# A batched matmul whose last store moves behind its critical sections, and whose second load of b moves to ScalarE's queue

## The chip, the cores and the metric

One core of a Trainium2 chip. The metric is the device time of one execution in microseconds (us); "ratio" is the mean time of one kernel's fast runs over the mean of the other kernel's fast runs of the same rounds, so it is not quite the ratio of the medians that are quoted. In the experiments the ratios come out when each kernel's first run, the profiled one, is left out; the medians and differences have it in, so the two can differ by some 0.1 us.

## The reference

```python
batch, m, k, n = 16, 512, 512, 512        # a: (batch, m, k), b: (batch, n, k), float32
np.matmul(a, b.transpose(0, 2, 1)).astype(np.float32)
```

Sixteen products of 512 x 512 matrices. 33.5 MB are read and 16.8 MB written.

## The kernel before

The batches are taken in pairs. A load brings two batches of a or of b (2 MB); loads 0, 2, 4, ... are of a and 1, 3, 5, ... of b. VectorE casts to bf16, TensorE transposes and multiplies, ScalarE evicts the products to `ob`, and stores of 1 MB carry them out. The streams of all engines stand in one large critical section, in which the framework inserts no waits and the kernel counts semaphores itself. A second small section at the end waits for the last store. These are the parts that matter here:

```python
    NL = 7                                 # slots for loads
    NO = 7                                 # slots for outputs
    STORES = "SSSSOSOSOSSOOOOOO"           # GpSimd: S stores, O hands a free output slot to ScalarE
    SW = 5
    LATE = {11: (8, 9), 13: (10, 11), 15: (12, 13)}
    # ... (cut)
    with tc.tile_critical(no_gpsimd_drain=True):
        # ... (cut: buffers, semaphores, load(), landed())
        def store(n):
            engine = nc.gpsimd if n < STORES.count("S") else nc.sync
            engine.wait_ge(s_out, n + 1)
            engine.dma_start(
                out[n].rearrange("(p j) n -> p j n", j=J), ob[:, n % NO]
            ).then_inc(landed(n)[0], 16)

        load(0)
        load(1, nc.scalar)
        for n in range(2, NL):
            load(n)
        for n in range(2 * pairs):
            nc.sync.wait_ge(s_ld[n % NL], 16 * (n // NL + 1)).then_inc(s_go, 1)
            if n > 0 and n + NL - 1 < 2 * pairs:
                load(n + NL - 1)           # waits until VectorE has cast what was in the slot
            for m in LATE.get(n, ()):
                store(m)
        store(batch - 2)
        store(batch - 1)
        for n in range(batch - NO, batch - 1):
            nc.sync.wait_ge(*landed(n))
        # ... (cut: GpSimd's, VectorE's, ScalarE's and TensorE's streams)

    with tc.tile_critical(no_gpsimd_drain=True):
        nc.sync.wait_ge(*landed(batch - 1))
```

Of the kernel before, what the change touches and what calls it, by code (L numbers as in the profile page):

```python
# [10 lines left out]
def kernel(  # L11
# [6 lines left out]
    nc = tc.nc  # L18
    P = 128
    batch, M, K = a.shape  # L20
    _, N, _ = b.shape
    J = M // P
# [6 lines left out]
    NL = 7  # L29
    NO = 7  # L30
# [7 lines left out]
    def sbuf(name, shape, dtype):  # L38
        return ctx.enter_context(nc.sbuf_tensor(name, shape, dtype))
# [4 lines left out]
    with tc.tile_critical(no_gpsimd_drain=True):  # L44
# [8 lines left out]
        ob = sbuf("ob", [P, NO, J, N], f32)  # L53
# [27 lines left out]
            out=ident[:], in_=ident[:], compare_op=mybir.AluOpType.not_equal, fill=1.0,  # L81
# [6 lines left out]
        def load(n, engine=nc.sync):  # L88
            u, slot = n // 2, n % NL
            src = (a if n % 2 == 0 else b)[2 * u:2 * u + 2].rearrange(  # L90
                "e (p j) k -> (e p) j k", j=2 * J
            )
            if n >= NL:

                nc.sync.wait_ge(s_cd, n - NL + 2)
            engine.dma_start(ld[:, slot], src).then_inc(s_ld[slot], 16)

        def landed(n):

            if n < STORES.count("S"):  # L100
                return s_st[n % SW], 16 * (n // SW + 1)

            slot = (n - STORES.count("S") + 2) % NL
            return s_ld[slot], 16 * (len(range(slot, 2 * pairs, NL)) + 1 + (n - STORES.count("S") >= NL))
# [7 lines that stand above are left out]

        load(0)
        load(1, nc.scalar)
        for n in range(2, NL):
            load(n)
        for n in range(2 * pairs):
            nc.sync.wait_ge(s_ld[n % NL], 16 * (n // NL + 1)).then_inc(s_go, 1)
# [3 lines left out]
            for m in LATE.get(n, ()):  # L122
                store(m)
        store(batch - 2)
        store(batch - 1)
        for n in range(batch - NO, batch - 1):
            nc.sync.wait_ge(*landed(n))


        n_st = n_of = 0  # L130
# [20 lines left out]
        with nc.Fori(0, pairs, engines=[dve]) as u:  # L151
            for x, (h, w, s_c, s_w) in enumerate(
# [4 lines left out]
                if x == 0:  # L157
# [3 lines left out]
                    out=h[:, :J, :], in_=src[:, :J, :HK]  # L161
                ).then_inc(s_cd, 1)
                nc.vector.tensor_copy(  # L163
                    out=h[:, J:, :], in_=src[:, J:, :HK]
                ).then_inc(s_c, 1)
                nc.vector.tensor_copy(out=w[:], in_=src[:, :, HK:]).then_inc(s_w, 1)  # L166
            for ko in range(KO):
# [5 lines left out]
                if ko == 1:  # L173
# [3 lines left out]
                    out=tb[:, ko, :],  # L177
# [4 lines left out]
        act = nc.scalar.engine  # L182
# [4 lines left out]
        with nc.Fori(0, pairs, engines=[act]) as u:  # L187
            for ko in range(KO):
# [5 lines left out]
                for e in range(2):  # L194
                    c = nc.scalar.copy(  # L195
                        out=ta[:, ko, e * J * P:(e + 1) * J * P].rearrange(
                            "k (j p h) -> k j p h", j=J, h=2
                        ),
# [5 lines left out]
            for e in range(2):  # L204
                take(s_of, 1)
                dst = ob[:, bass.ds((u * 2 + e) % NO, 1)].rearrange("m o j n -> m (o j) n")
                for j in range(J):
                    if j < J - 1:
                        nc.scalar.wait_ge(s_mm, j + 1)
                    else:  # L210
# [3 lines left out]
                        out=dst[:, j, :].rearrange("m (p j) -> m p j", j=2 * J),  # L214
# [50 lines left out]
                                t.then_inc(s_mm, 1)  # L265


    with tc.tile_critical(no_gpsimd_drain=True):
        nc.sync.wait_ge(*landed(batch - 1))


# [28 lines left out]
```

## Time and profile before

| | us |
|---|---|
| median of 6 runs | 125.48 (125.31 to 125.68) |
| span of the profiled run | 123.55 |
| first packet of data | 1.94 |
| last semaphore of the last store | 122.22 |
| from there to the end of the span | 1.33 |

The prediction below shows the slices, the stretches and the waits on which the reading rests. In the rows of slices each digit is the busy share, in tenths, of one of 40 equal slices of the span. "DMA share" is the mean busy share of the 16 DMA engines. A transfer has landed when the last increment of its semaphore has come; most transfers here get 16, one from each DMA engine. The exit of the second section shows as records of SyncE's sequencer at the line that opens it, L268. The view of that line has: line, engine (a "q" marks the sequencer), operation, count, shortest/median/longest in ns, first and last start in us.

```profile
L268 SPq NOP  x2: 13/13/13, 120.3 to 122.6; - x2
L268 SPq EVENT_SEMAPHORE  x1: 17/17/17, 122.4 to 122.4; - x1
L268 SPq DRAIN  x1: 7/7/7, 122.5 to 122.5; - x1
```

The first NOP, at 120.3 us, is the entry. Signal, drain and second NOP, at 122.4, 122.5 and 122.6 us, are the exit. They last 7 to 17 ns each, but they come one after the other behind the landing at 122.22 us, the signal 0.15 us after the branch before it, the others at distances of some 0.08 us. What they cost is the distance.

### The profile page before, as it was taken

How to read it: one execution, taken by the hardware profiler on the slowest of the kernel's cores; microseconds unless marked ns; L12 is line 12 of the kernel's file. 1: busy time of each engine (PE TensorE's matmuls, PEld its weight loads, DVE VectorE, ACT ScalarE, POOL GpSimd, SP SyncE). 2: the span in 40 equal slices, each digit the busy share in tenths (PEclk: the TensorE clock that was granted, in tenths of full speed). 3: DMA queues.
4: the chain of work that ended last, by engine and by line, in shares of the span. 5: the costliest groups of instructions: out<-in, count | busy, mean ns of one | idle time of the engine just before them, and what ended most of it. 6: DMA issues, size and time to landing. Idle time of an engine off the chain costs nothing. (4 is left out here: it accounts for less than half of the span.)

```text
span 123.5 us, 2364 instructions
## 1 busy us (share of the span) xinstructions
PE 90.7 (73%) x768; PEld 55.8 (45%) x768; DVE 67.9 (55%) x96; ACT 68.1 (55%) x130; POOL 5.9 (5%) x14
## 2 busy tenths in 40 slices
PE   0000089999899999989998999899999946994000
PEld 0000079546734774476467447644764535441000
DVE  0000597891898389568928991894787078400000
ACT  4000063458946885595769558937876069555000
POOL 2000000000000160001010230000000000000000
PEclk9999999999999999999999999999999999999955
DMA  4999999999999999999999999999999999999990
GB/s 127 419 446 435 424 424 430 424 424 424 430 430 435 424 403 385 461 390 427 454 400 454 424 414 454 411 432 446 416 438 419 416 427 422 430 424 427 430 385 11
DMA packets 4608, 50.33 MB, mean 407 GB/s; under 512 B 512, under 2 KB 512, under 8 KB 512
## 3 DMA queue, kind: packets, MB, share of 16 engines
q1 hardware_dynamic: 3312, 39.85, 76.2%
q0 software_dynamic: 1152, 8.39, 16.1%
q10 hardware_dynamic: 144, 2.10, 4.3%
HBM read 33.55 MB, written 16.78 MB: 407 GB/s over the span
## 5 line engine op out<-in xcount | busy, mean ns | idle before, releaser
L255 PE MATMUL ps<-tb,ta 128*128 128x512 bf16 x256 | 57.8, 379 | 0.5
L213 ACT COPY ob<-ps 128x512 f32 x64 | 34.5, 588 | 28.5 <-PE ps L255 24.6
L195 ACT COPY ta<-tp 128x512 bf16<-128x512 bf16 x64 | 32.8, 610 | 15.4 <-PE tp L236 15.4
L255 PEld LDWEIGHTS ps<-tb,ta 128*128 128x128 bf16 x256 | 24.1, 97 | 30.7 <-issue 4.0
L236 PE MATMUL tp<-ident,ha 128*128 128x128 bf16 x256 | 19.6, 230 | 19.3 <-PEq L141 19.3
L236 PEld LDWEIGHTS tp<-ident,ha 128*128 128x128 bf16 x256 | 16.6, 103 | 23.1 <-issue 21.3
L176 DVE COPY tb<-tp 128x1024 bf16<-128x1024 bf16 x32 | 21.2, 684 | 4.8 <-DVEq L141 4.8
L236 PE MATMUL tp<-ident,hb 128*128 128x128 bf16 x256 | 18.1, 227 | 2.2 <-PEq L141 2.2
L236 PEld LDWEIGHTS tp<-ident,hb 128*128 128x128 bf16 x256 | 16.1, 102 | 2.6 <-issue 2.6
L160 DVE CAST ha<-ld 128x1024 bf16 x8 | 5.5, 686 | 13.7 <-DVEq L141 13.7
L171 DVE COPY ha<-wa 128x2048 bf16<-128x2048 bf16 x8 | 5.5, 692 | 13.6 <-DVEq L141 13.6
L166 DVE CAST wa<-ld 128x2048 bf16 x8 | 9.8, 1227 | 0.0
L166 DVE CAST wb<-ld 128x2048 bf16 x8 | 9.7, 1218 | 0.0
L160 DVE CAST hb<-ld 128x1024 bf16 x8 | 5.5, 688 | 6.4 <-DVEq L141 6.4
L109 POOL DMA_DIRECT2D out_dram<-ob x8 | 5.2, 655 | 65.2 <-DMA ld<-in_b_dram 41.1
L175 DVE COPY hb<-wb 128x2048 bf16<-128x2048 bf16 x8 | 5.5, 684 | 0.1
L163 DVE CAST ha<-ld 128x1024 bf16 x8 | 5.5, 686 | 0.0
L163 DVE CAST hb<-ld 128x1024 bf16 x8 | 5.5, 683 | 0.0
L186 ACT ACT_TABLE_LOAD x1 | 1.3, 1283 | 1.5 <-SPq L44 1.5
L80 POOL TENSOR_SCALAR_AFFINE_SELECT ident<-ident 128x128 bf16<-128x128 bf16 x1 | 0.3, 282 | 0.2 <-POOL ident L78 0.2
L78 POOL MEMSET ident<- 128x128 bf16 x1 | 0.2, 204 | 0.5 <-SPq L44 0.5
L186 ACT COPY one<-const-float32-1.0 128x1 f32<-128x1 f32 x1 | 0.2, 191 | 0.0
(4 smaller groups left out, 0.4 us busy)
## 6 DMA issues: line engine op xcount, KB each, us to landing
ld<-in_a_dram SPq DMA_DIRECT2D x8, 2048.0 KB, 26.3
ld<-in_b_dram SPq DMA_DIRECT2D x7, 2048.0 KB, 29.8
out_dram<-ob POOLq DMA_DIRECT2D x8, 1024.0 KB, 29.0
out_dram<-ob SPq DMA_DIRECT2D x8, 1024.0 KB, 19.6
ld<-in_b_dram ACTq DMA_DIRECT2D x1, 2048.0 KB, 12.2
```

What stands on the lines that cost most here:

```text
L109: engine.dma_start(out[n].rearrange("(p j) n -> p j n", j=J), ob[:, n % NO]).then_inc(landed(n)[0], 16)
L160: nc.vector.tensor_copy(out=h[:, :J, :], in_=src[:, :J, :HK]).then_inc(s_cd, 1)
L163: nc.vector.tensor_copy(out=h[:, J:, :], in_=src[:, J:, :HK]).then_inc(s_c, 1)
L166: nc.vector.tensor_copy(out=w[:], in_=src[:, :, HK:]).then_inc(s_w, 1)
L171: nc.vector.tensor_copy(out=ha[:], in_=wa[:]).then_inc(s_ca, 1)
L175: nc.vector.tensor_copy(out=hb[:], in_=wb[:]).then_inc(s_cb, 1)
L176: nc.vector.tensor_copy(out=tb[:, ko, :], in_=tp[:, 2 + ko % 2].rearrange("k j p -> k (j p)"),).then_inc(s_eb, 1)
L186: nc.scalar.copy(out=one[:], in_=nc.const_aps.tensor(1.0, (P, 1), f32))
L195: c = nc.scalar.copy(out=ta[:, ko, e * J * P:(e + 1) * J * P].rearrange("k (j p h) -> k j p h", j=J, h=2), in_=tp[:, ko % 2, :, e * HP:(e ...
L213: c = nc.scalar.copy(out=dst[:, j, :].rearrange("m (p j) -> m p j", j=2 * J), in_=ps[:, j, :].rearrange("m (j p) -> m p j", j=2 * J),)
L236: t = nc.tensor.transpose(tp[:, 2 * x + g, j, :], h[:, j, g * P:(g + 1) * P], ident[:])
L255: t = nc.tensor.matmul(ps[:, j, :], ta[:, ko, (e * J + j) * P:(e * J + j + 1) * P], tb[:, ko, :].rearrange("k (j p) -> k j p", j=2 * J)[:, ...
```

## The change

The intent is a shorter end: the last store becomes a plain transfer of the framework after both sections, so that the framework's closing wait stands for it and no section has to be left afterwards. ScalarE, idle by then, takes the waits for the stores before it. Besides this the second load of b (load 3) goes to ScalarE's queue, as the first one does already.

```diff
         load(0)
         load(1, nc.scalar)
-        for n in range(2, NL):
+        load(2)
+        load(3, nc.scalar)
+        for n in range(4, NL):
             load(n)
 ...
         store(batch - 2)
-        store(batch - 1)
-        for n in range(batch - NO, batch - 1):
-            nc.sync.wait_ge(*landed(n))
 ...
-    with tc.tile_critical(no_gpsimd_drain=True):
-        nc.sync.wait_ge(*landed(batch - 1))
+    with tc.tile_critical(sync_engine=act, no_gpsimd_drain=True):
+        for n in range(batch - NO, batch - 1):
+            nc.scalar.wait_ge(*landed(n))
+    waits = nc.cur_bb.bb.instructions[-1]
+    last = nc.sync.dma_start(
+        out[batch - 1].rearrange("(p j) n -> p j n", j=J), ob[:, (batch - 1) % NO]
+    )
+    tc.add_manual_dep(
+        last.ins,
+        waits.name,
+        mybir.DependencyInfo(mybir.DependencyClass.NoSync, mybir.DependencyReason.DATA),
+        reason="order of issue",
+    )
```

## The prediction

> **What bounds the kernel now.** I read the page first, then the stretches, the chain, and the waits of SyncE's queue. The page's slices settle the large question: this kernel is bound by its transfers.
>
> ```profile
> PE   0000089999899999989998999899999946994000
> DVE  0000597891898389568928991894787078400000
> DMA  4999999999999999999999999999999999999990
> HBM read 33.55 MB, written 16.78 MB: 407 GB/s over the span
> ```
>
> The 16 DMA engines are busy from the first slice to the last but one, while TensorE and VectorE have holes and end three to six slices early. 50.33 MB are moved. In steady state the bandwidth row stays near 425 GB/s, so the bytes alone are worth 50.33 / 0.425 = 118.4 us of the 123.5 us span. What remains, about 5 us, is the head and the tail. The table by stretches places them (columns: stretch, length, busy time and count of PE, PEld, DVE, ACT, POOL, then clock, DMA share, GB/s):
>
> ```profile
> 0.00:1.90 1.90, 0.00 (x0) 0.00 (x0) 0.00 (x0) 0.42 (x1) 0.69 (x6) 1.00 0.00 0
> 1.90:2.90 1.00, 0.00 (x0) 0.00 (x0) 0.00 (x0) 0.99 (x2) 0.00 (x0) 1.00 1.06 279
> 2.90:13.00 10.10, 0.00 (x0) 0.00 (x0) 0.00 (x0) 0.06 (x1) 0.00 (x0) 1.00 1.02 435
> 13.00:23.00 10.00, 7.22 (x68) 6.52 (x68) 8.06 (x12) 4.11 (x8) 0.00 (x0) 1.00 0.99 423
> ...
> 112.00:120.20 8.20, 0.69 (x4) 0.10 (x1) 0.00 (x0) 1.09 (x2) 0.00 (x0) 0.83 1.00 424
> 120.20:121.80 1.60, 0.00 (x0) 0.00 (x0) 0.00 (x0) 0.00 (x0) 0.00 (x0) 0.50 0.08 31
> 121.80:123.50 1.70, 0.00 (x0) 0.00 (x0) 0.00 (x0) 0.00 (x0) 0.00 (x0) 0.50 0.00 0
> ```
>
> Nothing moves before 1.9 us. From there to 120.2 us the share is 0.99 to 1.06, that is, all engines are always at work. In 120.2 to 121.8 us it is 0.08, a little over one engine in 16: one DMA engine ends about 1.3 us after the other fifteen (in the records of packets its last data ends at 121.75 us, the others' between 120.1 and 120.7). Then 1.7 us in which nothing is moved. These last 3.3 us are the only part of the end that an instruction could shorten.
>
> The chain of work confirms that compute isn't the end. Its last piece in order of time is
>
> ```profile
> 112.89 0.59 ACT ob L213
> ```
>
> so ScalarE's last eviction ends at 113.48 us, ten microseconds before the end. What SyncE's queue waits for afterwards (engine, line, waited for: us in total, times, longest):
>
> ```profile
> SPq L127 <- DMA out_dram<-ob: 5.8, 3, 2.4
> SPq L109 <- ACT ob L213: 1.8, 1, 1.8
> SPq L295 <- DMA out_dram<-ob: 1.7, 1, 1.7
> ```
>
> L127 are the waits for the six stores before the last, inside the first section; L295 is the wait for the last store, in a section of its own. It lasts 1.7 us, so the last store is still under way when SyncE gets there.
>
> The sequencers' records give the end to the hundredth: the last store is issued at 113.50 us; L127 is done at 119.77; the first section is left with a join of all engines (119.81 to 120.36); the wait of L295 runs from 120.54 to 122.24, and the semaphore of the late DMA engine arrives at 122.22. From there: branch 122.28, signal 122.43, drain 122.52, NOP 122.59 (the second section is left), drain 122.63, drain 122.70, and then two barriers of all engines with a clearing of semaphores to 123.55. So 1.3 us follow the landing, and the first 0.4 us of it is the exit from the second section.
>
> **What the Trainium skill says.** "DMA: Bandwidth & Descriptors", section "Issuing engines are not separate DMA queues": DMAs of the scalar, sync and gpsimd engines run on the same 16 DMA engines and interleave; a second issuing engine saves the sequencer's issue time only. The trace agrees: loads 0 and 1, issued on SyncE and ScalarE 0.03 us apart, landed together at 13.29 and 13.12 us, at the same 435 GB/s that one queue alone gets later. The same page, "Queues, rings and completion order": each DMA engine takes turns between its queues packet by packet. This fits too, for two loads of 2 MB in some 10.2 us (2.9 to 13.1) is about twice the 4.89 us between landings of successive loads on one queue. "Perfetto Trace Analysis", section "Per-instruction lifecycle": waiting for a semaphore and its propagation lie outside the profiled window, which is why I read gaps between sequencer records and not their 7 to 33 ns durations.
>
> **The change part by part.**
>
> *Load 3 onto ScalarE's queue.* The number of bytes, of issues and of packets stays. One issue of 0.39 us (ScalarE's own now) moves from SyncE to ScalarE. It delays the table load at 1.48 us by some 0.4 us, but ScalarE's first real work is after 15 us: free. SyncE's loads 4 to 6 are issued 0.4 to 0.5 us earlier, into a queue with over 20 us of work: free. What changes is the order of landing. Now load 2 lands at 18.05 us and load 3 at 22.93. With turns between the two queues, both land near 22.9 to 23.1 us. Does anyone want load 2 earlier? The records of VectorE say no: it works at pair 0 until its loop comes round, and takes the signal for load 2 at 23.05 us, its first cast for pair 1 being at 23.43. So pair 1 starts 0 to 0.2 us later. Load 8, which waits for that cast (issued at 24.14), moves by as much; loads 4 to 7, 8 MB or 19.6 us of work, stand before it. Worth on the end: 0, give or take 0.1 us.
>
> *The waits for stores 9 to 14 move to ScalarE.* ScalarE is done at 113.48 us, so it can sit in them until 119.77 us at no cost; its section's exit, some 0.5 us, ends near 120.3, still 1.9 us before the landing. Off the path.
>
> *The last store behind the sections.* SyncE must first leave the first section. That exit waits for all engines' drains, ScalarE's at 113.48 us being the last, and took 119.96 to 120.36 us on the old trace, 0.4 us. So the store is issued near 113.9 to 114.1 us and not 113.50. This is hidden: the store before it holds the same queue until 118.0 us (landing of its first DMA engines), and from issue to first packet ScalarE's first load took 1.0 us, SyncE's 1.9. Even at 1.9 us it is ready at 116.0, 2 us early. The data still end at 120.2 us, and the late engine at 121.75.
>
> *The end.* Landing at 122.22 as before. The wait belongs to the framework's closing drain, so branch, signal, drain and NOP of the second section are gone from the path: instead of 122.24 to 122.63 to the closing drain, one hop of 0.06 us between adjacent records. Saved: 0.39 - 0.06 = 0.33 us. The two barriers, 0.9 us, stay.
>
> Sum: 0 + 0 + 0 - 0.33 = -0.33 us, so 125.49 - 0.33 = 125.16, and I say 125.15 us.
>
> **The rivals.**
>
> *The last store is held back.* If the framework sets it behind the waits of the second section and not only behind the first, it is issued at 119.8 us or later, when the queue is empty. Then 1.0 us to the first packet, 2.45 us of data (between landings of successive stores: 115.6, 118.0, 120.5) and 0.5 us to the semaphore put the landing at 123.8 to 125, 1.5 to 2.8 us later: 126.6 to 128. For it: the diff needs a dependence by hand to get the order it wants. Against: that dependence is one of order of issue without a semaphore, and the section holds instructions of ScalarE alone. I give this 1 in 20.
>
> *The late DMA engine changes its lag.* It gathers its 1.2 us from slow packets: the first ones (up to 1.45 us for 16 KB against 0.61) and those around 45 us, when GpSimd's stores begin. Two queues in use until 23 us may shift which engine suffers. If all ended together the time would fall by 1.2 us; it can also grow. For it: the time of the very end hangs on that one engine. Against: the three runs of before differ by only 0.2 us, so the lag recurs, and both its sources are untouched. This gives the range its width.
>
> *Compute becomes the bound through the later load 2.* Pair 1 would have to slip by more than the backlog, which is 19.6 us early and 6.7 us (120.2 - 113.5) at the end. A slip of 0.2 us vanishes. I give it nothing.
>
> **Range and chances.** The one certain term is -0.33 us with an error of 0.15; head and middle add perhaps 0.2, the late engine 0.3. Low 124.7, high 125.6. Two per cent would be 2.5 us: a gain of that size is not there, because only 3.3 us after 120.2 are not transfer at full rate, and the closing barriers with the receipt take half; a loss needs the first rival at its worst. Faster 0.01, same 0.97, slower 0.02.
>
> **What would show it.** Right: the slices of DMA as before; loads 2 and 3 landing within 0.5 us of each other near 23 us; VectorE's first cast for pair 1 by 23.7 us; the last store issued before 114.5 us; the landing near 122.2 us, and 0.9 to 1.0 us from there to the end of the span instead of 1.3. Wrong: a gap in the DMA row after 118 us (the store was held), a DMA share in the last stretch very different from 0.08 (the late engine), or as many records as before between the landing and the first closing drain (the framework's own wait costs what the section's exit did).

## The result

The changed kernel took 125.26 us (median of 6 runs, 124.99 to 125.48) against 125.48 us. The ratio is 0.9979 with a 95% interval of 0.9962 to 0.9995, a gain of 0.27 us by the means; in us the interval is a gain of 0.06 to 0.48. The time alone thus tells a gain of 0.33 us from none, but not from one of 0.1; the traces below do. The predicted time was 125.15 us, the range 124.7 to 125.6, the class "within 2%": all hold.

On the page of the changed kernel the large picture is as it was:

```profile
PE   0000079999899999989998999899999929997000
DMA  4999999999999999999999999999999999999990
q1 hardware_dynamic: 3168, 37.75, 72.3%
q10 hardware_dynamic: 288, 4.19, 8.3%
```

The transfers still fill every slice but the ends. The queue of ScalarE (q10) carries 288 packets, two loads, where it carried one (144 packets). The stretches at the end of the changed kernel:

```profile
112.00:120.20 8.20, 1.34 (x7) 0.39 (x4) 0.00 (x0) 1.53 (x3) 0.00 (x0) 0.71 1.01 427
120.20:121.80 1.60, 0.00 (x0) 0.00 (x0) 0.00 (x0) 0.00 (x0) 0.00 (x0) 0.50 0.09 36
121.80:123.40 1.60, 0.00 (x0) 0.00 (x0) 0.00 (x0) 0.00 (x0) 0.00 (x0) 0.50 0.00 0
```

There is no gap before 120.2 us, so the last store was not held back, and the share of 0.09 after it is again mostly one late DMA engine. What SyncE's queue waits for after 112 us, and the exit of the second section, now read:

```profile
SPq L306 <- DMA out_dram<-ob: 7.7, 1, 7.7
SPq L44 <- PEq L44: 0.9, 1, 0.9
SPq L44 <- ACTq L44: 0.7, 1, 0.7
```

```profile
L268 ACTq NOP  x2: 14/14/14, 114.3 to 120.8; - x2
L268 ACTq EVENT_SEMAPHORE  x1: 17/17/17, 120.6 to 120.6; - x1
L268 ACTq DRAIN  x1: 14/14/14, 120.7 to 120.7; - x1
```

SyncE leaves the large section early (two waits of 0.9 and 0.7 us for the drains of TensorE and ScalarE), issues the store at 114.31 us and sits in the framework's closing wait for 7.7 us. The exit of the second section is ScalarE's now and ends at 120.8 us, 1.6 us before the landing at 122.44 us. After the landing come the wait's end at 122.49, two drains at 122.53 and 122.59 us and the two barriers. The end, taken from the records of the two traces ("fifteenth" and "sixteenth" here and in later tables are in the order in which the DMA engines finish, not the engines' numbers):

| | before | changed |
|---|---|---|
| ScalarE's last eviction ends | 113.47 | 114.12 |
| last store issued | 113.50 | 114.31 |
| fifteenth DMA engine done (semaphore) | 121.00 | 121.37 |
| sixteenth DMA engine done (semaphore) | 122.22 | 122.44 |
| from landing to the end of the span | 1.33 | 1.00 |
| span | 123.55 | 123.44 |

The end is 0.33 us shorter. In this pair of profiles the landing is 0.22 us later, which single runs cannot tell from scatter; over the runs of the first series of experiments, the spans of before have a mean of 123.73 us and the changed kernel's are all 123.4.

### The profile page after: what moved, and what is told of

It is laid out like the page before. It is cut to its first block, busy times and chain, and to the rows that moved or that the text cites. A ratio compares the mean times of both kernels' runs of the same rounds, so it can differ in the third digit from the quotient of the medians.

```text
span 123.4 us, 2365 instructions
## 1 busy us (share of the span) xinstructions
PE 91.1 (74%) x768; PEld 56.0 (45%) x768; DVE 68.1 (55%) x96; ACT 68.2 (55%) x130; POOL 5.8 (5%) x14
```

## The experiments

My theory: the whole gain is the exit of a section taken from behind the landing, 0.33 us, and load 3's queue is worth nothing. The rival: the loads on two queues make the gain. A second question is how much room the last store has, since it is now issued later. A third is the DMA engine that ends some 1.1 us after the others, which no part of the change touches but on which the time of the end hangs.

In the tables below "difference" is mean minus mean of the kernel before in the same rounds.

### The two parts alone, and one section more

`after_again` is the changed kernel. `tail_only` takes back the loads:

```diff
-        load(2)
-        load(3, nc.scalar)
-        for n in range(4, NL):
+        for n in range(2, NL):
```

`load_only` is the kernel before with only this part of the change added. `third_section` is the kernel before with its last section written twice:

```diff
     with tc.tile_critical(no_gpsimd_drain=True):
         nc.sync.wait_ge(*landed(batch - 1))
+
+    with tc.tile_critical(no_gpsimd_drain=True):
+        nc.sync.wait_ge(*landed(batch - 1))
```

Expected of `after_again`: 

> The changed kernel once more, on the chip of the next three runs. My theory: 0.2 to 0.4 us below the kernel before (0.9979 before), all of it from the 0.33 us between the landing of the last store and the end of the span. Rival: the gain comes from the loads on two queues, and the end gives nothing.

Expected of `tail_only`: 

> The end of the changed kernel with the loads of the kernel before (only load 1 on ScalarE's queue). My theory: 0.33 us below before, as the whole change or a little better, since the late landing of load 2 is spared; 0.95 to 1.05 us from the landing to the end. Rival (the loads make the gain): same as before, 0.0 us.

Expected of `load_only`: 

> Load 3 on ScalarE's queue, and the end of the kernel before. My theory: within 0.15 us of before, either sign; loads 2 and 3 landing within 0.3 us of each other near 23.4 us. Rival (the loads make the gain): 0.2 to 0.3 us below before.

Expected of `third_section`: 

> The kernel before with one more section at the end that waits again for the last store, which has landed: it pays one more entry and exit. My theory: a section's exit behind the landing costs 0.33 us and its entry 0.2, so 0.4 to 0.6 us above before. Rival (sections cost nothing there): 0.0 us.

| run | median us | ratio to before (95%) | difference | landing to end of span |
|---|---|---|---|---|
| after_again | 125.24 | 0.9980 (0.9967 to 0.9994) | -0.30 | 1.00 |
| tail_only | 125.08 | 0.9962 (0.9949 to 0.9976) | -0.45 | 1.00 |
| load_only | 125.45 | 0.9996 (0.9982 to 1.0010) | -0.08 | 1.33 |
| third_section | 126.36 | 1.0067 (1.0053 to 1.0081) | +0.79 | 1.98 |

The rival falls: with the new end alone the gain is there, with the loads alone it isn't. The last column, from each trace, is 1.00 us wherever the new end is and 1.33 us wherever the old one is. The added section shows the same cost with the sign turned. Its entry and exit come after the landing (122.33 us):

```profile
L271 SPq NOP  x2: 13/13/13, 122.8 to 123.3; - x2
L271 SPq EVENT_SEMAPHORE  x1: 17/17/17, 123.2 to 123.2; - x1
L271 SPq DRAIN  x1: 7/7/7, 123.3 to 123.3; - x1
```

They stretch the end by 0.65 us (1.98 - 1.33), a little more than the 0.6 that I took as the most. The time rose by 0.79 us, outside the 0.4 to 0.6 that I expected. The rest is outside the span: the time less the span is 2.06 us in this kernel's runs (mean of five) and 1.83 us in those of before. What it consists of I can't see.

### How much room the last store has

`hold_14` and `hold_13` are the kernel before with the last store issued only after the landing of an earlier store (number 14 or 13), on purpose:

```diff
-        store(batch - 1)
-        for n in range(batch - NO, batch - 1):
+        for n in range(batch - NO, 15):        # 14 in hold_13
+            nc.sync.wait_ge(*landed(n))
+        store(batch - 1)
+        for n in range(15, batch - 1):         # 14 in hold_13
             nc.sync.wait_ge(*landed(n))
```

Expected of `hold_14`: 

> The kernel before, with the last store issued only after the store before it has landed. It puts my first rival of the prediction to the test, by doing on purpose what I feared the framework would do. I said 1.5 to 2.8 us in the prediction for this case (1.0 us to the first packet, 2.45 us of data, 0.5 us to the semaphore, from 119.8 us on). If the last store has no slack at all, it would be more, some 4 us.

Expected of `hold_13`: 

> The kernel before, with the last store issued one store earlier than in the run with the longer hold: after the landing of the last but two, near 117.4 us instead of 113.5. My theory: the store before it keeps the DMA engines at work to 118.0 us and the late one to 119.2, and the first packet comes 1.0 us after the issue, so at most 0.4 us is lost and, if the late engine decides, nothing: 0.0 to 0.3 us above before. Rival (every us of delay of the last store counts): 3 to 4 us above before.

| run | last store issued | landing | sixteenth after fifteenth | median us | ratio (95%) | difference |
|---|---|---|---|---|---|---|
| before (profile) | 113.50 | 122.22 | 1.21 | | | |
| hold_13 | 117.85 | 122.64 | 0.94 | 125.49 | 0.9992 (0.9973 to 1.0011) | 0.0 |
| hold_14 | 119.98 | 123.82 | 0.03 | 126.97 | 1.0118 (1.0101 to 1.0136) | +1.49 |

Issuing the store 4.4 us later costs nothing that the runs can tell (the interval is -0.34 to +0.14 us). Issuing it 6.5 us later costs 1.5 us. The stretches near the end show why; first `hold_13`, then `hold_14` (the last two columns are DMA share and GB/s):

```profile
118.00:119.00 1.00, 0.00 (x0) 0.00 (x0) 0.00 (x0) 0.00 (x0) 0.00 (x0) 0.50 0.40 164
119.00:120.00 1.00, 0.00 (x0) 0.00 (x0) 0.00 (x0) 0.00 (x0) 0.00 (x0) 0.50 1.10 459
120.00:121.00 1.00, 0.00 (x0) 0.00 (x0) 0.00 (x0) 0.00 (x0) 0.00 (x0) 0.50 1.04 426
121.00:122.00 1.00, 0.00 (x0) 0.00 (x0) 0.00 (x0) 0.00 (x0) 0.00 (x0) 0.50 0.13 49
```

```profile
119.00:120.00 1.00, 0.00 (x0) 0.00 (x0) 0.00 (x0) 0.00 (x0) 0.00 (x0) 0.50 0.02 8
120.00:121.00 1.00, 0.00 (x0) 0.00 (x0) 0.00 (x0) 0.00 (x0) 0.00 (x0) 0.50 0.31 131
121.00:122.00 1.00, 0.00 (x0) 0.00 (x0) 0.00 (x0) 0.00 (x0) 0.00 (x0) 0.50 0.93 393
122.00:123.00 1.00, 0.00 (x0) 0.00 (x0) 0.00 (x0) 0.00 (x0) 0.00 (x0) 0.50 0.97 393
```

In `hold_13` most DMA engines do stand idle between 118 and 119 us (share 0.40), and the time is unchanged all the same: the late engine, done with the store before only at 119.8 us, has no gap, and it alone sets the landing (122.64 us; the fifteenth comes at 121.70). In `hold_14` all are empty, all start the last store together, and the lag is gone with the wait. This is the price of the rival that I gave 1 in 20; the changed kernel's store, 0.8 us later than before, is far inside the room.

### The late DMA engine

`sync_stores` is the changed kernel with GpSimd's eight stores on SyncE's queue:

```diff
-    SW = 5
+    SW = 8
-    LATE = {11: (8, 9), 13: (10, 11), 15: (12, 13)}
+    LATE = {5: (0, 1), 7: (2, 3), 9: (4, 5), 11: (6, 7), 12: (8, 9), 13: (10, 11), 15: (12, 13)}
 ...
-            engine = nc.gpsimd if n < STORES.count("S") else nc.sync
+            engine = nc.sync
 ...
-            if what == "S":
-                store(n_st)
-                n_st += 1
-            else:
+            if what == "O":
```

`last_120` is the changed kernel with its last store cut in two, and `last_skip` is `tail_only` with it cut in four (the dependence by hand moves into the loop; it is cut here):

```diff
-    last = nc.sync.dma_start(
-        out[batch - 1].rearrange("(p j) n -> p j n", j=J), ob[:, (batch - 1) % NO]
-    )
+    for r in (slice(0, 120), slice(120, 128)):   # last_skip: 0:96, 96:117, 117:124, 124:128
+        last = nc.sync.dma_start(
+            out[batch - 1].rearrange("(p j) n -> p j n", j=J)[r], ob[r, (batch - 1) % NO]
+        )
```

Expected of `sync_stores`: 

> The changed kernel with the eight stores that GpSimd issued put on SyncE's queue; GpSimd only waits. It asks whether the DMA engine that ends 1.1 us late in every profile, and the slow packets at 45 to 47 us, come from GpSimd's way of issuing. If so: late engine within 0.5 us of the others, landing near 120.8 us and 1.3 to 1.8 us below before. Rival (an engine is late whoever issues): lag of 1 us as before, and the time of the changed kernel (0.3 us below before), or more if one queue in strict order holds the loads back.

Expected of `last_120`: 

> The changed kernel with the last store cut in two transfers, of 120 and of 8 partitions. By the Trainium skill (DMA: Bandwidth & Descriptors, on how many engines a DMA uses) 120 partitions go to the 15 lowest engines and 8 to the 8 lowest, so the sixteenth engine gets none of the last store. If the late engine is the sixteenth: the last landing 0.8 to 1.1 us earlier, time 1.1 to 1.4 us below before. If it is another: landing 0 to 0.6 us later than in the changed kernel (one packet more on eight engines, 0.31 us, and one issue more).

Expected of `last_skip`: 

> The better end with the loads of before, and the last store cut in four: 96, 21, 7 and 4 partitions. By the Trainium skill's rule for the number of engines, 96 go to all sixteen (6 each), 21 and 7 to the seven lowest (4 more), 4 to the four lowest (1 more). The run with 120 and 8 partitions showed that the late engine is one of the eight lowest; the skill (same page, latency table) says that engines 7 and 15 are usually slower. If the late one is the eighth of them, it has 6 packets instead of 8 (0.61 us less) and the lowest ones up to 11 (0.92 us more): last landing near 121.8 us and not 122.4, lag of the sixteenth under 0.4 us, time 0.3 to 0.5 us below the uncut version. If the late one is among the seven lowest: landing 0.6 to 0.9 us later, near 123.2 us, time 0.6 to 1.0 us above the uncut version.

| run | landing | sixteenth after fifteenth | median us | ratio (95%) | difference |
|---|---|---|---|---|---|
| sync_stores | 126.87 | 0.01 | 129.74 | 1.0348 (1.0308 to 1.0387) | +4.35 |
| last_120 | 123.13 | two transfers, see text | 125.62 | 1.0004 (0.9988 to 1.0020) | +0.14 |
| last_skip | 123.24 | four transfers, see text | 126.12 | 1.0054 (1.0034 to 1.0073) | +0.67 |

`sync_stores` was a miss as a kernel and answers only half of its question. Its page shows a hole near the end that no other kernel has:

```profile
ACT  3000066459567956876069260893409915894630
DMA  4999999999999999999999999999999999993094
```

Early stores stand in one queue behind loads (the first is issued at 37.72 us and lands at 64.88; before, 42.81 and 55.15), outputs' slots come free late, ScalarE and with it all compute fall behind, and between 115 and 121 us the DMA engines run dry (share 0.22). The lag of 0.01 us at the very end says nothing, since everybody started the last store together, as in `hold_14`. But the semaphores of the stores before that hole can be read: in the one at 115 to 118 us the sixteen come spread over 2.9 us, from 115.61 to 118.49, with 0.61 us between the last two. For the store that lands at that time in the traces of before and of the changed kernel, fourteen come within 0.5 us, and the last lags the one before it by 1.18 and 1.05 us. So a single late engine is a trait of the runs with GpSimd's stores, but in the one trace without them the engines drift apart too. The slow packets go elsewhere rather than away: their excess over the usual time, summed over all packets, is 0.5 us in 45 to 50 us against 7.5 us before, but 5.3 us in 55 to 60. All of this excess but 0.01 us is in packets of loads, and it comes shortly before the first store's own packets move (slow from 45.0 us and first store packet at 47.03 before; 58.6 and 61.49 here, with more at 65 to 70 and 80 to 85 us). So the stores' packets are not slow, and GpSimd's issuing is not needed for loads to be. Nor does that excess set the lag: over the thirteen profiles with GpSimd's stores it runs from 1.8 us (`last_skip`) to 9.5 us (`last_120`) in 45 to 50 us, while at the store before the last the sixteenth engine comes 1.04 to 1.64 us after the fifteenth, 1.13 us in `last_skip`.

`last_120` locates the late engine. The transfer of 8 partitions lands 0.30 us after the other one (122.83 and 123.13 us; 0.69 us later than in the changed kernel's trace, just over the 0.6 that I allowed). When all other packets are done, at 121.25 us, five are left that follow one another, ending at 121.53, 121.84, 122.15, 122.45 and 122.76 us; the two landings come some 0.38 us after the last two. So the late engine has a share of both transfers. By the Trainium skill (DMA: Bandwidth & Descriptors, section "Why a DMA increments its semaphore by 16 and not by 1") 8 partitions go to the eight lowest engines, so the late one is one of these. The trace agrees with the page's account of the count: of the 120-partition transfer one increment comes at 114.62 us, right after the issue, and fifteen between 120.73 and 122.83. In `last_skip` the late engine appears in the transfers of 21 and 7 partitions (last semaphores 122.94 and 123.24 us), not in the one of 4, whose last comes at 122.45. By the same rule it is, in this run, the fifth, sixth or seventh. I had bet on the eighth and lost, at 1.0 us above `tail_only_2` by the means; by dealing its packets to the seven lowest I loaded the very engine that I meant to spare. By this rule every transfer on few engines goes to the lowest, so a cut spares the late one only in transfers of four partitions or fewer, which all load the lowest four; I ran none. Why it is late stays open.

### The section's exit without a second section, and the loads once more

`one_section` is the kernel before with the wait for the last store inside the large section:

```diff
-        for n in range(batch - NO, batch - 1):
+        for n in range(batch - NO, batch):
             nc.sync.wait_ge(*landed(n))
 ...
-    with tc.tile_critical(no_gpsimd_drain=True):
-        nc.sync.wait_ge(*landed(batch - 1))
```

`tail_only_2` and `after_3` repeat two kernels side by side.

Expected of `one_section`: 

> The kernel before without its second section: the wait for the last store ends the first section, so that the exit of the large section, with its join of all engines, lies behind the landing. From the trace of before: 0.60 us from the branch that leaves the large section (119.81 us) to the end of its join with the hop to the next record (120.41), against 0.36 us for the exit of the small one (122.28 to 122.63). My theory: 0.2 to 0.3 us above before, and 1.5 to 1.7 us from the landing to the end of the span instead of 1.33. Rival (only the number of sections counts, as the third section's 0.65 us in the trace might suggest): 0.3 us or more below before.

Expected of `tail_only_2`: 

> The end of the changed kernel with the loads of the kernel before, a second time, on one chip with the changed kernel, to see whether the second load on ScalarE's queue costs the 0.16 us by which this one led. If it does: 0.1 to 0.25 us below the changed kernel again. If that was chance: within 0.1 us of it.

Expected of `after_3`: 

> The changed kernel, a third time, as the partner of the run before it: 0.2 to 0.35 us below the kernel before.

| run | median us | ratio to before (95%) | difference | landing to end of span |
|---|---|---|---|---|
| one_section | 125.97 | 1.0031 (1.0016 to 1.0047) | +0.45 | 1.93 |
| tail_only_2 | 125.18 | 0.9973 (0.9956 to 0.9989) | -0.35 | 1.00 |
| after_3 | 125.36 | 0.9986 (0.9970 to 1.0001) | -0.21 | 1.00 |

The direction for `one_section` was right, the size too small: 0.60 us more behind the landing, where I had 0.2 to 0.3. The exit itself is only 0.18 us longer than the small section's (0.593 us from the landing to SyncE's first closing drain against 0.417). The other 0.42 us are here (first `one_section`, then the same view of before):

```profile
L291 POOLq DRAIN  x3: 34/113/714, 122.9 to 124.2; - x3
L291 SPq DRAIN  x3: 7/7/7, 123.1 to 123.8; - x3
```

```profile
L295 POOLq DRAIN  x3: 34/113/714, 120.1 to 123.3; - x3
L295 SPq DRAIN  x3: 7/7/7, 122.6 to 122.9; - x3
```

GpSimd's first closing drain takes 714 ns and starts when the section that it takes part in is left: at 120.1 us before, under the wait for the last store, and at 122.9 us here, in the open: SyncE's second drain is at 123.17 us, and the barrier's next record, GpSimd's, comes only at 123.63; before they are 0.03 us apart. So the second section that the change takes off the path had a use: it let GpSimd drain early. The change keeps this, as its large section ends at 112 to 114 us.

`tail_only` led the changed kernel by 0.15 us in both series by the means (125.11 and 125.17 against 125.26 and 125.32), while `load_only` was 0.08 us ahead of before. The first speaks for a small price of load 3's place and the second for a small gain. All that can be said is that the place of load 3 is worth little: the means say -0.08 to +0.15 us, and the interval of `load_only` alone runs from -0.23 to +0.13. The kernel with the new end and the old loads is the fastest that was run, ahead of before in both series clear of the interval, and ahead of the changed kernel by a margin that these runs don't settle.

## Why the prediction was right

**The bound.** Transfers at full rate, from 1.9 to 120.2 us, before and after: shown by the slices and the stretches of both kernels.

**The end.** Predicted 0.33 us from the exit that goes away, with 0.9 to 1.0 us left behind the landing; measured 1.33 to 1.00 us, the same in every trace of either end. ScalarE's waits ended with their section's exit at 120.8 us, where I had 120.3, and stayed off the path. The mean differences of the changed kernel (-0.27, -0.30, -0.21 us) lie at or a little under the size, those of `tail_only` (-0.45, -0.35) a little over; of the five only that of `after_3` is not clear of zero by its interval (ratio up to 1.0001). That the predicted 125.15 us lies within 0.11 us of the measured median is in part luck, as the landing alone moved between 122.29 and 122.58 us over the five traces with the new end.

**Load 3.** Predicted 0, give or take 0.1 us; `load_only` -0.08 us. The details were a little off. The first two loads, on two queues, ran at 435 GB/s; I called that the rate of one queue alone, which then shows 423 to 430. Load 2 landed at 23.47 us and not by 23.1, and VectorE's first cast for pair 1 came at 23.91 us, where I had allowed until 23.7 us. Here is that cast and the idle time before it in the changed kernel's timeline:

```profile
21.92 1.29 DVE L175 COPY tb<-tp 128x1024 bf16<-128x1024 bf16 x2 [0.46 <-DVEq L140]
23.91 0.69 DVE L159 CAST ha<-ld 128x1024 bf16 x1 [0.70 <-DVEq L140]
```

VectorE does now stand idle for 0.70 us there: pair 1 starts 0.48 us later, not 0 to 0.2. Load 8 is issued at 24.63 instead of 24.14 us. The backlog hides it, as the DMA share shows no gap.

**The last store.** Issued at 114.31 us, later than the 113.9 to 114.1 that I worked out, because ScalarE's last eviction itself ended 0.65 us later in that run. The exit of the section was over-sized: I took 0.4 us from the old trace, and from the end of the eviction to the issue it is 0.18 us in each of the three traces of the changed kernel (the other engines' steps of the join had run before). The two errors partly cancel. The room was larger than the 2 us that I counted: `hold_13` shows that 4.4 us cost nothing. I had counted from the fifteen engines, and the late one decides.

**The rivals.** The held-back store did not happen; `hold_14` shows that it would have cost 1.5 us, the low end of what I said. The late engine kept its lag (1.21 and 1.07 us). I had it gather its lag from slow packets, the first ones and those near 45 us. That part is not shown: the second source shrinks to 1.8 us in `last_skip` and the lag stays, and no run tests the first. One trace, `sync_stores`, hints that a single engine's lag comes with GpSimd's stores; the slow packets of loads come without them too.

## What to carry to other kernels

In a kernel bound by transfers, the end to shorten is what follows the last semaphore: list the sequencers' records after it, and let every exit, join and drain that does not need the last transfer happen under it. Cutting up the last transfer, or reordering loads in a full queue, did not help here. Before moving a transfer later, find its room by holding it back on purpose: here it was free at 4.4 us, with the slowest DMA engine still at work on the store before, and cost 1.5 us at 6.5 us, when all had run dry.

## What the Trainium skill lacked or had wrong

- "DMA: Bandwidth & Descriptors", latency table, says that DMA engines 7 and 15 are usually slower. Here one engine ends 1.07 to 1.55 us after the other fifteen in the profiles of before, of the changed kernel and of the runs with one part of it, and where it was located (`last_120`, `last_skip`) it is by the page's own rule for few partitions neither of those two: it had packets of the transfers of 8, 21 and 7 partitions and none of that of 4, so the fifth to seventh.
- The same page gives a fixed cost of about 2.0 us per DMA, from a fit to GpSimd's path, and no such total for SyncE's. In `hold_14`, where a 1 MB store of SyncE's queue meets empty engines, issue to landing took 3.84 us, of which 2.45 us are data at the rate of the other stores and 1.4 us come on top: 0.83 us of it before the first packet, some 0.35 us from the last packets to the last semaphore, and 0.2 us by which the packets took longer than 2.45 us.
- No page gives the price of a critical section at the end of a kernel: 0.33 us for an exit behind the last landing (1.33 against 1.00 us), 0.65 us for an entry and an exit, and with the added one another 0.2 us outside the span (2.06 against 1.83 us).
- No page tells that GpSimd's closing drain takes 714 ns and begins when the last section that GpSimd takes part in is left; `one_section` paid 0.42 us for it.
